# A two-layer decoder trunk in split float32: each unit of weights is placed at one of 32 byte offsets inside its tiles

## The chip, the cores and the metric

The kernel runs on one core of a Trainium2 chip. The metric is device time of one execution in microseconds (us); lower is better. A core has a matrix engine (TensorE, in the profile PE for the matmuls and PEld for the loads of the stationary operand), a vector engine (VectorE, DVE), a scalar engine (ScalarE, ACT), GpSimd (POOL) and SyncE (SP), which issues the DMAs. The engines run at the same time and wait for each other by semaphores. They share an on-chip memory of 128 partitions (SBUF); matmuls write to another one (PSUM).

## The reference

Two layers over 512 tokens of width 1024, all in float32. A layer is a token mixer (Mamba-2 SSD in the first, HGRN2 in the second), a layer norm, an MLP with squared ReLU, a second layer norm and a gated embedding:

```python
for i in range(DEPTH):
    mix = ssd_mixer(x, ...) if i % 2 == 0 else hgrn2_mixer(x, ...)
    h = layer_norm(DEEPNORM_ALPHA * x + mix, ln_g[i, 0], ln_b[i, 0])
    h = layer_norm(DEEPNORM_ALPHA * h + sq_relu_mlp(h, mlp_w1[i], mlp_w2[i]), ln_g[i, 1], ln_b[i, 1])
    x = h + jax.nn.sigmoid(h @ ple_w_gate[i]) * (p[i] @ ple_w_proj[i])
```

The bulk of it are matrix products: the input and output projections of the two mixers, the MLP (1024 to 4096 to 1024, `a = relu(h @ w1); (a * a) @ w2`) and the gates.

## The kernel before

Every product with weights is made from three matmuls. An operand is split in two parts, hi (the value rounded to the reduced format float32r) and lo (what is left), and the product is hi·hi + hi·lo + lo·hi. `mm3` (L116 to L119) issues the three; its lines L117, L118 and L119 hold most of the TensorE instructions of the profile. Each writes 128 partitions by 512 columns (some 256) of PSUM.

Weights come in units of 128 partitions by 1024 float32 values, 512 KB each. `unit` (L100 to L105) loads one into a tile `raw` of the pool `raws` (3 buffers), and `split` (L107 to L115) makes two tiles of it: ScalarE casts it into `whi` (L111), VectorE subtracts and writes `wlo` (L113). The pools `whip` and `wlop` have 5 buffers each, used in rotation, so the cast of a unit waits until TensorE has done the last matmul on the unit that had the buffer five units earlier. In the MLP some units are sums of weights, formed on VectorE in tiles `r` (`weight_sums`, L280 to L299) and split in the same way. 292 units are split in one execution.

A unit is used in one of two roles. In `project` (and `qf`) a slice of 128 columns of the unit is the stationary operand and the activations move (`pj<-b,whi` in the profile: out, moving, stationary). In `out_part`, `block_product`, the gates and `vg` the activations are stationary and a slice of 512 or 256 columns of the unit moves (`pj<-whi,b`). The activations lie in tiles of the pool `b8` (9 buffers of 8192 bytes in each partition), split in hi and lo as well. Two of the seven block operands of the MLP (`s3` and `s4`, read in `block_product`, L301) lie in tiles `blk` of the stage's own pool instead; `ones_r`, a constant, is the stationary operand of the column sums in the HGRN2 stage (L794), whose moving operand lies in `b8`.

The order of the instructions on each engine is made by a scheduler from the program's order and the priorities (`high_priority`); in the HGRN2 stage TensorE's order is written out by hand.

Where a tile lies is fixed when the program is built. The pools stand one behind the other in each partition: constants, `raws`, `whip`, `wlop`, `b8`, `acc`, `w4` (tiles a and b), small ones, a `pad` of 64 bytes, and the pool of the stage. In the program before the change:

| tiles | first byte in a partition | bytes in each | first byte modulo 256 |
|---|---|---|---|
| ones_r | 5472 | 512 | 96 |
| raw (3) | 6112 | 4096 | 224 |
| whi (5) | 18400 | 4096 | 224 (all five) |
| wlo (5) | 38880 | 4096 | 224 (all five) |
| b8 (9) | 59360 | 8192 | 224 (all nine) |
| acc | 133088 | 16384 | 224 |
| a, b | 149472, 157664 | 4096 | 224 |
| blk (2) and the other tiles of a stage | 166496 on | 8192 for blk | 96 |

The slices that a matmul takes out of these tiles begin at multiples of 512 bytes in them, so modulo 256 they begin where the tile does.

Of the kernel before, what the change touches and what calls it, by code (L numbers as in the profile page):

```python
# [9 lines left out]
F32R = mybir.dt.float32r  # L10
# [5 lines left out]
P = 128  # L16
# [26 lines left out]
def trunk(ctx: ExitStack, tc, a):  # L43
# [4 lines left out]
    whip = pool("whip", 5)  # L48
    wlop = pool("wlop", 5)
# [8 lines left out]
    psm = pool("psm", 1, space=PSUM)  # L58

    uid = [0]  # L60

    def nm(s):
        uid[0] += 1
        return f"{s}_{uid[0]}"

    def mk(p, shape, tag, dt=F32, **kw):
        return p.tile(list(shape), dt, tag=tag, name=nm(tag), **kw)

    def f32(t):
        return t.bitcast(F32)  # L70
# [29 lines left out]
    def unit(src, lead=LEAD):  # L100
        n = src.shape[1]
        with tc.high_priority(offset=lead):
            raw = mk(raws, [P, 1024], "raw")
            nc.sync.dma_start(raw[:, :n], src)
        return split(raw[:, :n], lead)  # L105

    def split(f, lead=LEAD):  # L107
        n = f.shape[1]
        with tc.high_priority(offset=lead):
            hi = mk(whip, [P, 1024], "whi", F32R)  # L110
            nc.scalar.copy(hi[:, :n], f)  # L111
            lo = mk(wlop, [P, 1024], "wlo", F32R)
            nc.vector.tensor_sub(lo[:, :n], f, f32(hi[:, :n]))  # L113
        return hi, lo

# [46 lines left out]
    cols, at = {}, 0  # L162
# [138 lines left out]
    def block_product(w, blk, first, after=None):  # L301
# [6 lines left out]
        def product(x, f, name, start, i, j):  # L308
            us = [split(v) if f in (t1, t2, t3, t4) else unit(v) for v in f]
            if start:  # L310
                banks[name] = [bank(psy, "py%d" % c) if name == "x" else bank(psj, "pj") for c in range(2)]
            t = blk[x]
            for c in range(2):
                ps = banks[name][c]
                sl = slice(c * P, (c + 1) * P)
                for k in range(4):
                    hi, lo = us[k // 2]
                    ks = slice((k % 2) * 512, (k % 2 + 1) * 512)
                    w_ = hi[:, ks], lo[:, ks]
                    mm3(ps, t[:, 0, k, sl], t[:, 1, k, sl], *w_, start and k == 0, k == 3, skip_group_check=True)  # L320
                d = acc[:, 2 * i + c, j * 512 : (j + 1) * 512]
                if (i, j) in seen:
                    nc.vector.tensor_add(d, ps, d)  # L323
                else:
                    nc.vector.scalar_tensor_tensor(d, d, ALPHA, ps, ALU.mult, ALU.add)
            seen.add((i, j))
# [719 lines left out]
```

## Time and profile before

| | |
|---|---|
| median of three timed runs | 1490.86 us (1487.89 to 1492.02) |
| the profiled execution: its own time | 1487.04 us |
| its span, first to last instruction | 1485.3 us |
| split, ScalarE (L111): 292 casts | 239.1 + 67.1 us busy |
| split, VectorE (L113): 292 subtractions | 278.5 + 78.1 us busy |
| 128x512 matmuls on weights | 5064 |
| 128x256 matmuls on weights | 1200 |
| DMA | 175.10 MB, mean 118 GB/s |

In the profile a busy time is the time in which an engine has at least one instruction under way. Matmuls overlap in TensorE's pipeline, so a matmul's own duration (389 ns in a smooth stretch) is longer than the time from its start to the start of the next one, which this document calls a step. "Idle before" is time in which the engine of that group had nothing to do just before its instructions, with what ended it. A chain of waits is the sequence of work that ended last, followed back from the last instruction.

### The profile page before, as it was taken

What the parts mean: (1) busy time and instruction counts of PE and PEld (TensorE: products, weight loads), DVE (VectorE), ACT (ScalarE), POOL (GpSimd) and SP (SyncE); (2) the same over time, 40 slices, a digit from 0 to 9 for tenths busy, and PEclk for the clock granted to TensorE, in tenths of its full rate; (3) what the DMA queues carried; (4) which work ended last, traced back from release to release, by engine and by line L of the source; (5) the groups of instructions that cost most, each with busy time, mean ns of one, the idle gap of its engine ahead of it and who ended that gap; (6) DMA issues with size and microseconds to landing.
All of it is one profiled execution on the core that took longest, in us unless ns stands there. A gap on an engine that the chain in (4) does not pass through costs nothing.

```text
span 1485.3 us, 19598 instructions
## 1 busy us (share of the span) xinstructions
PE 1463.3 (99%) x7720; PEld 1219.7 (82%) x7720; DVE 1086.6 (73%) x1672; ACT 725.3 (49%) x1020; POOL 0.9 (0%) x9
## 2 busy tenths in 40 slices
PE   8999999999999999999999999999999999999998
PEld 5888888888788888887778998989788888888777
DVE  7998677787956768687954767768786776767883
ACT  6777455563264444544534463543346454444542
POOL 0000000000000000000000000000000000000000
PEclk9999999999999999999999999999999999999999
DMA  6433223334333434444223212222423434444222
GB/s 249 159 113 101 103 97 116 100 111 141 115 114 128 156 128 145 139 154 140 80 77 102 97 58 73 71 71 86 167 90 114 142 131 152 143 142 156 99 86 72
DMA packets 48526, 175.10 MB, mean 118 GB/s; under 512 B 5393, under 2 KB 5905, under 8 KB 48305
## 3 DMA queue, kind: packets, MB, share of 16 engines
q1 hardware_dynamic: 48432, 173.84, 35.0%
q8 instruction: 61, 1.00, 0.3%
q14 instruction: 33, 0.26, 0.1%
HBM read 171.66 MB, written 2.16 MB: 117 GB/s over the span
## 4 chain that ended last, share of the span: by engine, by line
PE 92%; DVE 6%; DMA 1%; ACT 1%; issue 1%; SPq 0%; ACTq 0%
PE pj L117 24%; PE pj L118 23%; PE pj L119 23%; PE py L117 4%; PE py L118 4%; PE py L119 4%; DVE wlo L113 2%; PE py L784 1%; PE py L593 1%; PE pm L563 1%; PE py L598 1%; PE pt L208 1%; PE py L794 1%; PE py L829 1%; ACT whi L111 1%
## 5 line engine op out<-in xcount | busy, mean ns | idle before, releaser
L111 ACT CAST whi<-raw 128x1024 fp32r<-128x1024 f32 x228 | 239.1, 1049 | 329.6 <-PE pj L118 176.0
L117 PE MATMUL pj<-b,whi 128*128 128x512 f32 (+1 forms) x1024 | 391.4, 384 | 3.0 <-ACT whi L111 1.6
L113 DVE TENSOR_TENSOR wlo<-raw,whi 128x1024 fp32r<-128x1024 f32 x228 | 278.5, 1222 | 154.8 <-ACT whi L111 153.9
L118 PE MATMUL pj<-b,whi 128*128 128x512 f32 (+1 forms) x1024 | 387.7, 379 | 0.0
L119 PE MATMUL pj<-b,wlo 128*128 128x512 f32 (+1 forms) x1024 | 387.6, 379 | 0.0
L117 PE MATMUL pj<-whi,b 128*128 128x512 f32 (+1 forms) x712 | 252.0, 355 | 0.5 <-ACT sg L416 0.5
L118 PE MATMUL pj<-wlo,b 128*128 128x512 f32 (+1 forms) x712 | 249.8, 351 | 0.8 <-DVE wlo L113 0.8
L119 PE MATMUL pj<-whi,b 128*128 128x512 f32 (+1 forms) x712 | 249.8, 351 | 0.0
L117 PEld LDWEIGHTS pj<-b,whi 128*128 128x128 f32 x1024 | 192.9, 189 | 38.9 <-ACT whi L111 3.0
L119 PEld LDWEIGHTS pj<-b,wlo 128*128 128x128 f32 x1024 | 193.0, 189 | 35.7 <-DVE wlo L113 1.2
L118 PEld LDWEIGHTS pj<-b,whi 128*128 128x128 f32 x1024 | 193.2, 189 | 33.9 <-issue 1.9
L118 PEld LDWEIGHTS pj<-wlo,b 128*128 128x128 f32 x712 | 134.7, 189 | 18.2 <-DVE wlo L113 2.0
L117 PEld LDWEIGHTS pj<-whi,b 128*128 128x128 f32 x712 | 134.6, 189 | 17.8 <-ACT sg L416 0.7
L119 PEld LDWEIGHTS pj<-whi,b 128*128 128x128 f32 x712 | 134.6, 189 | 17.0 <-issue 0.2
L111 ACT CAST whi<-r 128x1024 fp32r<-128x1024 f32 x64 | 67.1, 1049 | 113.6 <-PE pj L118 90.9
L113 DVE TENSOR_TENSOR wlo<-r,whi 128x1024 fp32r<-128x1024 f32 x64 | 78.1, 1221 | 31.8 <-ACT whi L111 31.7
L119 PE MATMUL py<-whi,b 128*128 128x512 f32 x224 | 87.1, 390 | 0.0
L117 PE MATMUL py<-whi,b 128*128 128x512 f32 x192 | 75.1, 391 | 1.9 <-DVE acc L323 1.9
L118 PE MATMUL py<-wlo,b 128*128 128x512 f32 x192 | 74.7, 389 | 0.0
L498 DVE SCALAR_TENSOR_TENSOR cv<-pj,cst,cv 128x511 f32<-128x511 f32 (+2 forms) x72 | 53.3, 744 | 5.8 <-ACT cv L495 5.2
L119 PEld LDWEIGHTS py<-whi,b 128*128 128x128 f32 x224 | 42.0, 188 | 8.9 <-DVE b L394 0.3
L117 PEld LDWEIGHTS py<-whi,b 128*128 128x128 f32 x192 | 36.0, 188 | 10.7 <-DVE acc L323 3.3
(218 smaller groups left out, 1865.3 us busy)
## 6 DMA issues: line engine op xcount, KB each, us to landing
raw<-in_w SPq DMA_DIRECT2D x112, 512.0 KB, 3.5
r<-in_w SPq DMA_DIRECT2D x64, 512.0 KB, 3.8
raw<-in_wssd SPq DMA_DIRECT2D x40, 512.0 KB, 3.5
a<-csd SPq DMA_DIRECT2D x16, 512.0 KB, 4.1
raw<-in_wso SPq DMA_DIRECT2D x16, 512.0 KB, 3.5
raw<-in_wg SPq DMA_DIRECT2D x16, 512.0 KB, 3.5
raw<-in_whvg SPq DMA_DIRECT2D x16, 512.0 KB, 3.5
raw<-in_whq SPq DMA_DIRECT2D x16, 512.0 KB, 3.4
```

The source lines that it names most:

```text
L111: nc.scalar.copy(hi[:, :n], f)
L113: nc.vector.tensor_sub(lo[:, :n], f, f32(hi[:, :n]))
L117: nc.tensor.matmul(out, sh, mh, start=start, stop=False, **kw)
L118: nc.tensor.matmul(out, sh, ml, start=False, stop=False, **kw)
L119: nc.tensor.matmul(out, sl, mh, start=False, stop=stop, **kw)
L208: nc.tensor.transpose(pt[:, j * P : (j + 1) * P], src[:, k * P : (k + 1) * P], ident)
L498: nc.vector.scalar_tensor_tensor(cv[:, d:], ps[:, : T - d], convw[:, i, k : k + 1], cv[:, d:], ALU.mult, ALU.add)
L563: nc.tensor.matmul(pst_[:, c * P : (c + 1) * P], btok[:, c, :], xw[:, c].rearrange("p h q -> p (h q)"), start=True, stop=True)
L593: nc.tensor.matmul(yd[64 * r : 64 * r + 64, sl], xdt[:, 2 * c + r, :], m[:, r, sl], start=True, stop=True)
L598: nc.tensor.matmul(yo[:, c * P : (c + 1) * P], pv[:, c - 1].rearrange("p h q -> p (h q)"), cm[:, c * P : (c + 1) * P], start=True, stop=True,)
L784: nc.tensor.matmul(pc[:, sl], kk[:, sl], q[:, sl], start=True, stop=True)
L794: nc.tensor.matmul(pc[:, :n], ones_r, hl[:, r, :n], start=r == 0, stop=r == 1)
```

## The change

Each split takes the next of 32 offsets, 0 to 31 values of 4 bytes, and uses it for both of its tiles. The tiles grow by 32 values, so that a unit of 1024 still fits at the last offset. Everything that reads a unit gets the shifted view.

```diff
     uid = [0]
+    places = [0]
...
     def split(f, lead=LEAD):
         n = f.shape[1]
         with tc.high_priority(offset=lead):
-            hi = mk(whip, [P, 1024], "whi", F32R)
+            at = places[0] % 32
+            places[0] += 1
+            hi = mk(whip, [P, 1056], "whi", F32R)[:, at : at + 1024]
             nc.scalar.copy(hi[:, :n], f)
-            lo = mk(wlop, [P, 1024], "wlo", F32R)
+            lo = mk(wlop, [P, 1056], "wlo", F32R)[:, at : at + 1024]
             nc.vector.tensor_sub(lo[:, :n], f, f32(hi[:, :n]))
         return hi, lo
```

## The prediction

> **What bounds the kernel.** I read the page first: busy times, the granted clock and the chain of waits.
>
> ```profile
> span 1485.3 us, 19598 instructions
> PE 1463.3 (99%) x7720; PEld 1219.7 (82%) x7720; DVE 1086.6 (73%) x1672; ACT 725.3 (49%) x1020; POOL 0.9 (0%) x9
> ...
> PEclk9999999999999999999999999999999999999999
> ...
> PE 92%; DVE 6%; DMA 1%; ACT 1%; issue 1%; SPq 0%; ACTq 0%
> ...
> L117 PE MATMUL pj<-b,whi 128*128 128x512 f32 (+1 forms) x1024 | 391.4, 384 | 3.0 <-ACT whi L111 1.6
> ```
>
> TensorE is busy for 1463.3 of 1485.3 us at an undiminished clock and is 92% of the chain; before the largest group of matmuls on weights it idled only 3.0 us. So the time is the number of matmuls times the step from one start to the next, plus 22.0 us of idle time. Matmuls overlap, so the duration in a group's row is not that step. The windows view of a smooth stretch gives it.
>
> ```profile
> core 0: us, PE busy (x) PEld busy (x) DVE busy (x) ACT busy (x) POOL busy (x), PEclk, DMA share, GB/s
> 425.00:475.00 50.00, 50.00 (x222) 41.41 (x221) 27.81 (x34) 25.26 (x33) 0.00 (x0) 1.00 0.35 116
> ```
>
> 222 matmuls touch these 50 us. The first began before the stretch; each lasts 0.389 us, so (50.00 + 0.39)/222 = 0.227 us a step, all of them 512 columns wide.
>
> Then I looked for the same matmul with its operands at other places. Here is the timeline of TensorE where one block product starts and ends:
>
> ```profile
> 481.60 0.39 PE L118 MATMUL pj<-b,whi 128*128 128x512 f32 x1
> 481.82 0.40 PE L119 MATMUL pj<-b,wlo 128*128 128x512 f32 x1
> 482.06 0.40 PE L117 MATMUL pj<-whi,blk 128*128 128x512 f32 x1
> 482.30 0.40 PE L118 MATMUL pj<-wlo,blk 128*128 128x512 f32 x1
> 482.53 0.39 PE L119 MATMUL pj<-whi,blk 128*128 128x512 f32 x1
> ...
> 487.41 0.40 PE L119 MATMUL pj<-whi,blk 128*128 128x512 f32 x1
> 487.64 0.39 PE L117 MATMUL pj<-b,whi 128*128 128x512 f32 x1
> ```
>
> From 482.06 to 487.64 there are 24 steps on blk: 5.58/24 = 0.2325 us, 5.5 ns more than 0.227, with no wait shown. Single steps reach 0.24 us (482.06 to 482.30), and the step that leads into the first of them (481.82 to 482.06) is long as well. The work is the same as for a tile in b8; the place is not. By the program's addresses b8, whi, wlo, a and b all begin 224 bytes past a multiple of 256, and blk begins 96 past one. Its stationary operand is thus 128 bytes apart, modulo 256, from the moving one; on all other matmuls on weights the two are 0 apart. One more tile read beside b8 begins at 96: ones_r.
>
> ```profile
> L117 PE MATMUL pj<-b,whi 128*128 128x512 f32 x52 | 20.2, 389 | 0.0
> ...
> L794 PE MATMUL py<-b,ones_r 128*128 128x512 f32 x32 | 10.1, 396 | 0.0
> L117 PE MATMUL py<-whi,blk 128*128 128x512 f32 x64 | 25.3, 396 | 0.0
> ```
>
> The first row is of the smooth stretch (425 to 475 us), the others of the whole span: both tiles at 96 show 396 ns against 389, in other stages and other lines. So the trace holds two states, 0 apart and 128 apart, and the second is dearer. This is what the forecast rests on.
>
> **The change, part by part.** It adds and removes no instruction, and on every engine the order is as before. It does three things.
>
> *The writes.* 292 splits write whi (ScalarE) and wlo (VectorE, which also reads whi) at an offset of 4 bytes times a counter modulo 32.
>
> ```profile
> L111 ACT CAST whi<-raw 128x1024 fp32r<-128x1024 f32 x228 | 239.1, 1049 | 329.6 <-PE pj L118 176.0 <-PE pj L119 104.4 <-PE py L119 26.0
> L113 DVE TENSOR_TENSOR wlo<-raw,whi 128x1024 fp32r<-128x1024 f32 x228 | 278.5, 1222 | 154.8 <-ACT whi L111 153.9
> ...
> L498 DVE SCALAR_TENSOR_TENSOR cv<-pj,cst,cv 128x511 f32<-128x511 f32 x24 | 17.9, 745 | 0.2
> L498 DVE SCALAR_TENSOR_TENSOR cv<-pj,cst,cv 128x509 f32<-128x509 f32 x24 | 17.8, 742 | 5.2 <-ACT cv L495 5.2
> L605 DVE SCALAR_TENSOR_TENSOR y<-xs,cst,py 128x512 f32<-128x512 f32 x16 | 11.9, 745 | 2.3 <-PE py L593 2.2
> L266 DVE TENSOR_TENSOR blk<-a,blk 128x512 fp32r<-128x512 f32 x16 | 11.0, 685 | 0.0
> L266 DVE TENSOR_TENSOR b<-a,b 128x512 fp32r<-128x512 f32 x32 | 22.0, 686 | 4.1 <-ACT b L265 4.1
> ...
> L265 ACT CAST blk<-a 128x512 fp32r<-128x512 f32 x16 | 9.9, 617 | 2.1 <-PE pj L119 2.1
> L265 ACT CAST b<-a 128x512 fp32r<-128x512 f32 x32 | 19.8, 620 | 6.8 <-DVE a L273 4.7 <-PE py L119 1.8
> ```
>
> The convolution (L498) reads and writes 4 and 12 bytes off on VectorE, 745 and 742 ns against 745 for the even L605: no cost. Operands 128 bytes apart cost neither VectorE (685 against 686) nor ScalarE (617 against 620) anything. ScalarE at an odd word has no row; bounds: 0 by VectorE's rows, and at worst a doubling, 292 x 1.049 = 306 us more on an engine busy for 725.3, still below TensorE. I take 0. What hides it is that the splits wait for a free buffer behind TensorE (the 329.6 us before the casts); without that cover each ns on a cast is 0.3 us in all.
>
> *The tiles grow* from 4096 to 4224 bytes, which is 16 x 256 + 128. The five buffers of whi begin 224, 96, 224, 96, 224 past a multiple of 256, those of wlo 96, 224, 96, 224, 96. All that is allocated behind them moves by 1280 bytes, a whole number of 256, so b8 stays at 224, blk and ones_r at 96. The growth alone would put half of the matmuls on weights 128 apart; hi and lo of one unit are always in different states.
>
> *The reads.* 6264 matmuls read whi or wlo, 3072 as the stationary and 3192 as the moving operand (5064 are 512 wide, 1200 are 256). Buffers and offsets together spread their distance modulo 256 over all 64 words. Before, 4680 of the wide ones were 0 apart and 384 (blk) 128. Listing the built program's matmuls, 2764 of the 5064 come to lie 64 or more bytes apart (the short way round), and 3845 do so or precede one that does. The step into the first blk matmul is long as well, so I count both.
>
> The price at distances between 0 and 128 is not in the trace. Its bounds:
> - growing evenly up to 5.5 ns at 128: the mean distance is 66.4 bytes, so 5064 x 5.5 x 66.4/128 = 14.4 us, less the 384 x 5.5 = 2.1 us that blk pays already: 12.3 us;
> - 5.5 ns wherever the distance is not 0 (4964 matmuls): 27.3 - 2.1 = 25.2 us;
> - 5.5 ns from half way on, both steps counted: 3845 x 5.5 = 21.1, less 2.1: 19.0 us;
> - the slowest step on blk, 0.24 against 0.227, everywhere: 4964 x 13 ns = 64.5, less 2.1: 62 us;
> - nothing at all: 0.
>
> I take 19 us: it uses the mean that was measured, and it lies between the first two. The narrow matmuls:
>
> ```profile
> L118 PE MATMUL pj<-wlo,b 128*128 128x256 f32 x272 | 76.8, 282 | 0.0
> ...
> L794 PE MATMUL py<-b,ones_r 128*128 128x256 f32 x16 | 3.1, 276 | 0.0
> ...
> L882 PE MATMUL py<-a,cm 128*128 128x128 f32 x64 | 11.0, 274 | 0.0
> L884 PE MATMUL py<-pv,xs 128*128 128x128 f32 x48 | 9.3, 275 | 0.0
> ```
>
> At 256 columns the pair 128 apart (ones_r) lasts 276 ns against 282, and at 128 columns a and cm, 128 apart, last 274 against 275 for pv and xs, 0 apart. So I put the 1200 narrow ones at 0; the ends are -6 ns (-7 us) and 5.5 ns (+7 us).
>
> The Trainium skill bears on this: "TensorE: Matmul & The Clock Gate", section "Step-by-step: what each phase is for", says that TensorE reads SBUF through two independent ports, one for the moving operand and one for the weight load. By that rule the distance could not matter and the sum would be 0; the blk steps of 0.2325 us against 0.227 speak against it, and the measurement decides.
>
> **Sum.** The profiled execution took 1487.0 us (span 1485.3), 3.8 below the median of 1490.86. 1487.0 + 19 = 1506.0; on the median's footing 1510.
>
> **Rivals.**
> *No effect.* The long steps belong to something else that blk and ones_r share (their absolute place, which does not change), and the offset as such is free as on VectorE. For it: the narrow rows. Against it: half the weight buffers come to lie at 96 too. 1491 us.
>
> *Faster.* A step has a fixed part, which distance 0 may make large:
>
> ```profile
> 406.43 0.28 PE L118 MATMUL pj<-b,whi 128*128 128x256 f32 x1
> ...
> 408.34 0.28 PE L118 MATMUL pj<-b,whi 128*128 128x256 f32 x1
> ```
>
> 16 steps in 1.91 us are 119 ns for 256 columns; 227 for 512 leaves 227 - 2 x (227 - 119) = 11 ns that do not grow with the width. If those are the weight read, begun at the same place as the moving read, being held up by it, then the distances with no such clash save up to 11 ns. It decides if more than half of the distances are free: 6264 x 11 x 0.5 = 34 us, 1456 us. Against it: at 128 apart the wide step is longer, not shorter.
>
> *Much slower.* Distances in between, or starts off a multiple of 16 bytes (2394 moving and 2304 stationary operands), cost more than 128 apart: at the slowest blk step everywhere 1491 + 62 = 1553 us. For it: 0.24 us does occur. Against it: the mean on blk is 0.2325.
>
> **How the numbers follow.** Forecast 0.62, its own range 1500 to 1525 (12 to 34 us); much slower 0.17; no effect 0.13; faster 0.08. A change under 0.3%, 4.5 us, can't be told from none here. Slower 0.79, same 0.13, faster 0.08. The range 1488 to 1552 takes in no effect and most of the dear case; outside stay the gain (0.08) and the dearer half of that rival (0.09).
>
> **What would show it.** Right: idle time on TensorE stays near 22 us while smooth stretches hold fewer matmuls (some 218 instead of 222 in 50 us); the step changes from unit to unit and stays near 0.227 where the operands are almost 0 apart; L111 and L113 keep 1049 and 1222 ns. Wrong: steps of 0.227 throughout (no effect), steps below 0.22 (faster), most at 0.24 or above (much slower), or longer casts that TensorE waits for, which I have put at nothing.

## The result and the profile after

| | before | after |
|---|---|---|
| median | 1491.44 us (4 runs, 1487.89 to 1493.23) | 1509.58 us (4 runs, 1508.86 to 1512.19) |
| ratio after / before | | 1.0134, 95% interval 1.0120 to 1.0147 |
| the profiled execution: own time, span | 1487.04, 1485.3 us | 1510.05, 1508.0 us |

The kernel became slower by 1.34%, 20 us of 1491.4. The forecast was 1510 us on the median's footing, where 1509.58 was measured, and 1506.0 for the profiled execution, which took 1510.05. The page of the changed kernel has these lines (busy time, share and count of each engine; the clock; the chain of waits; groups of instructions). The lines of code stand three further down than before: L120 to L122 are the three matmuls, L114 and L116 the split.

```profile
span 1508.0 us, 19598 instructions
PE 1485.9 (99%) x7720; PEld 1223.2 (81%) x7720; DVE 1086.8 (72%) x1672; ACT 724.5 (48%) x1020; POOL 0.9 (0%) x9
...
PEclk9999999999999999999999999999999999999999
...
PE 94%; DVE 4%; DMA 1%; ACT 1%; issue 1%; SPq 0%; ACTq 0%
...
L114 ACT CAST whi<-raw 128x1024 fp32r<-128x1024 f32 x228 | 238.9, 1048 | 344.2 <-PE pj L121 185.3
...
L116 DVE TENSOR_TENSOR wlo<-raw,whi 128x1024 fp32r<-128x1024 f32 x228 | 278.6, 1222 | 165.6 <-ACT whi L114 164.8
```

The 22.7 us that the span gained are busy time of TensorE: 1485.9 - 1463.3 = 22.6. Some 3 us of them are clock (an estimate): the mean granted clock was 0.999 in the profiled execution before and 0.997 in the one after, 0.002 x 1508. Executions of before with a lower granted clock are longer (medians in the runs below: 1489.8 us at 0.999, 1491.5 at 0.997, 1494.2 at 0.995), so a span alone is a poorer measure of the change than the ratio. VectorE and ScalarE do the same work in the same time (1222 and 1048 ns for a piece of a split, 1222 and 1049 before); they only wait longer for buffers, 344.2 us instead of 329.6 before the casts. The number of matmuls is the same, 7720. In the smooth stretch that the prediction used, the granted clock is 1.00 as before (third column from the end), and 216 matmuls touch it instead of 222:

```profile
425.00:475.00 50.00, 50.00 (x216) 40.44 (x215) 28.79 (x37) 26.74 (x36) 0.00 (x0) 1.00 0.35 115
```

So the step between matmuls grew. Two smooth stretches of the timeline, first and last matmul of each:

```profile
423.16 0.39 PE L120 MATMUL pj<-b,whi 128*128 128x512 f32 x1
...
456.45 0.39 PE L122 MATMUL pj<-b,wlo 128*128 128x512 f32 x1
...
235.64 0.39 PE L120 MATMUL pj<-whi,b 128*128 128x512 f32 x1
...
254.26 0.39 PE L122 MATMUL pj<-whi,b 128*128 128x512 f32 x1
```

In the first, weights are stationary: 143 steps in 33.29 us, 232.8 ns. In the second they move: 80 steps in 18.62 us, 232.75 ns. Before, both kinds took 227. This is the step that the prediction read off blk (232.5 ns).

For the rest of this document I take from each trace the start of every wide (512 columns) matmul on weights to the start of the next matmul, leave out those of 270 ns and more (waits), and give means. Before: 228.0 ns over 4821 steps; after: 232.7 over 4823. The narrow ones (256 columns, steps under 200 ns) went from 119.8 to 119.1.

### The profile page after: what moved, and what is told of

It reads as the page before. It is cut to its first block, busy times and chain, and to the rows that moved or that the text cites. A ratio compares the mean times of both kernels' runs of the same rounds, so it can differ in the third digit from the quotient of the medians.

```text
span 1508.0 us, 19598 instructions
## 1 busy us (share of the span) xinstructions
PE 1485.9 (99%) x7720; PEld 1223.2 (81%) x7720; DVE 1086.8 (72%) x1672; ACT 724.5 (48%) x1020; POOL 0.9 (0%) x9
## 4 chain that ended last, share of the span: by engine, by line
PE 94%; DVE 4%; DMA 1%; ACT 1%; issue 1%; SPq 0%; ACTq 0%
PE pj L120 24%; PE pj L121 24%; PE pj L122 24%; PE py L120 4%; PE py L122 4%; PE py L121 4%; PE py L787 1%; PE py L596 1%; DVE wlo L116 1%; PE pm L566 1%; PE py L601 1%; ACT whi L114 1%; PE py L797 1%; PE pt L211 1%; PE py L832 1%; DVE b L215 1%
## 5 line engine op out<-in xcount | busy, mean ns | idle before, releaser
L114 ACT CAST whi<-raw 128x1024 fp32r<-128x1024 f32 x228 | 238.9, 1048 | 344.2 <-PE pj L121 185.3
L120 PE MATMUL pj<-b,whi 128*128 128x512 f32 (+1 forms) x1024 | 395.8, 388 | 2.9 <-ACT whi L114 1.6
L116 DVE TENSOR_TENSOR wlo<-raw,whi 128x1024 fp32r<-128x1024 f32 x228 | 278.6, 1222 | 165.6 <-ACT whi L114 164.8
L121 PE MATMUL pj<-b,whi 128*128 128x512 f32 (+1 forms) x1024 | 392.0, 383 | 0.0
L122 PE MATMUL pj<-b,wlo 128*128 128x512 f32 (+1 forms) x1024 | 392.0, 383 | 0.0
L120 PE MATMUL pj<-whi,b 128*128 128x512 f32 (+1 forms) x712 | 254.2, 358 | 0.5 <-ACT sg L419 0.5
L122 PE MATMUL pj<-whi,b 128*128 128x512 f32 (+1 forms) x712 | 251.5, 353 | 0.0
L120 PEld LDWEIGHTS pj<-b,whi 128*128 128x128 f32 x1024 | 193.2, 189 | 42.8 <-ACT whi L114 3.2
L122 PEld LDWEIGHTS pj<-b,wlo 128*128 128x128 f32 x1024 | 193.3, 189 | 39.8 <-DVE wlo L116 1.2
L120 PEld LDWEIGHTS pj<-whi,b 128*128 128x128 f32 x712 | 134.4, 189 | 19.3 <-ACT sg L419 0.7
L122 PEld LDWEIGHTS pj<-whi,b 128*128 128x128 f32 x712 | 134.5, 189 | 18.7 <-issue 0.2
L114 ACT CAST whi<-r 128x1024 fp32r<-128x1024 f32 x64 | 67.2, 1049 | 117.7 <-PE pj L121 93.9
L116 DVE TENSOR_TENSOR wlo<-r,whi 128x1024 fp32r<-128x1024 f32 x64 | 78.1, 1221 | 34.8 <-ACT whi L114 34.7
L122 PE MATMUL py<-whi,b 128*128 128x512 f32 x224 | 88.2, 395 | 0.0
L120 PE MATMUL py<-whi,b 128*128 128x512 f32 x192 | 76.0, 396 | 1.8 <-DVE acc L326 1.8
L122 PEld LDWEIGHTS py<-whi,b 128*128 128x128 f32 x224 | 42.2, 188 | 10.0 <-DVE b L397 0.3
L120 PEld LDWEIGHTS py<-whi,b 128*128 128x128 f32 x192 | 36.1, 188 | 11.2 <-DVE acc L326 2.6
```

The lines of the kernel that those rows point to most:

```text
L120: nc.tensor.matmul(out, sh, mh, start=start, stop=False, **kw)
L121: nc.tensor.matmul(out, sh, ml, start=False, stop=False, **kw)
L122: nc.tensor.matmul(out, sl, mh, start=False, stop=stop, **kw)
```

## The experiments

Theories: **A**, the step is 227 ns where a matmul's two operands start at the same place modulo 256 and dearer at another distance; **B**, the absolute place counts; **C**, the change of place from unit to unit counts; **W**, starts that are not multiples of 16 bytes cost. All times are compared with the kernel before on the same chip.

| run | ratio, 95% interval | weights stationary | weights move, b8 stationary | weights move, blk stationary | narrow |
|---|---|---|---|---|---|
| before | | 227.6 | 227.7 | 232.8 | 119.8 |
| the change | 1.0134 (1.0120 to 1.0147) | 232.3 | 233.0 | 233.0 | 119.1 |
| E1 growth alone | 1.0087 (1.0072 to 1.0102) | 231.4 | 230.8 | 230.8 | 118.6 |
| E2 offsets alone | 1.0128 (1.0113 to 1.0143) | 232.1 | 232.9 | 233.7 | 119.3 |
| E3 weights 128 off | 1.0107 (1.0092 to 1.0122) | 232.7 | 232.8 | 227.5 | 118.7 |
| E4 all 128 off | 1.0001 (0.9991 to 1.0010) | 227.6 | 227.6 | 232.8 | 120.0 |
| E5 0 or 256 off | 0.9998 (0.9988 to 1.0008) | 227.6 | 227.7 | 232.8 | 119.8 |
| E6 weights 4 off | 1.0211 (1.0197 to 1.0225) | 232.4 | 237.3 | 236.3 | 121.6 |
| E7 weights 12 off | 1.0066 (1.0051 to 1.0082) | 231.1 | 229.2 | 230.7 | 117.3 |
| E8 blk and ones_r at 0 | 0.9993 (0.9984 to 1.0002) | 227.6 | 227.6 | 226.8 | 119.5 |
| E9 b8 4 off | 1.0196 (1.0180 to 1.0212) | 237.3 | 232.4 | 232.6 | 119.7 |
| E10 weights and b8 4 off | 1.0299 (1.0281 to 1.0317) | 237.6 | 237.6 | 236.3 | 122.5 |
| E11 as E8, narrow weights 12 off | 0.9958 (0.9943 to 0.9972) | 227.6 | 227.6 | 226.8 | 117.3 |

The four middle columns are mean steps in ns; in bytes, "off" is against the place before.

### E1 and E2: which part of the edit, the growth or the offsets

Both are edits to the changed kernel.

```diff
-            at = places[0] % 32
+            at = 0
```

> The tiles of whi and wlo grow to 4224 bytes as in the change, but every unit stays at offset 0. Of the 5064 wide matmuls on weights 2344 are then 128 bytes apart modulo 256 from their other operand and 2720 are 0 apart. Theory A (distance: any wide matmul whose two operands are not 0 apart, or that stands beside one, takes about 5.5 ns more): hi and lo of a unit are always in different states, so nearly every step is beside one; +15 to +25 us, a ratio of 1.010 to 1.017. Theory W (word place: the cost comes from starts that are not multiples of 16 or 32 bytes): no such start exists here; ratio 1.000. Theory C (change of place from unit to unit): places change in whole 128s; between the two.

```diff
-            hi = mk(whip, [P, 1056], "whi", F32R)[:, at : at + 1024]
+            hi = mk(whip, [P, 1088], "whi", F32R)[:, at : at + 1024]
...
-            lo = mk(wlop, [P, 1056], "wlo", F32R)[:, at : at + 1024]
+            lo = mk(wlop, [P, 1088], "wlo", F32R)[:, at : at + 1024]
```

> The 32 offsets as in the change, but in tiles of 4352 bytes (17 x 256), so that the growth adds no distance of 128: the distances are the offsets alone, 0 to 124 bytes, the same for hi and lo of a unit. Theory A with any distance other than 0 priced alike: +22 to +27 us, 1.015 to 1.018. Theory A with a price that grows evenly to 5.5 ns at 128: +13 us, 1.009. Theory W: the whole of the change, 1.013.

E1 gave 1.0087 and E2 1.0128, so either part alone makes most of the loss, and together they cost no more than the offsets alone. W by itself is out: in E1 every start is a multiple of 16 bytes. E1 came in just under what A promised (1.010 to 1.017). E2 lies under A's 1.015 to 1.018 as well and on W's 1.013, so its time alone doesn't tell the two apart. Its steps with weights stationary do: there every moving operand starts at a multiple of 16 bytes, and they grew all the same.

The trace of E1 tells which neighbours count. Where weights are stationary, by the state (0 or 128 apart) of the matmul before, the matmul itself and the one after, the mean steps are: 0,0,0 227.8 ns (471 steps); 1,0,0 228.9 (338); 0,0,1 232.4 (364); 0,1,0 233.3 (309). So a step is dear when its own matmul or the next one is off, and not on account of the one before. Where weights move the picture is less clear (229.6 for 0,0,0 on b8).

E2 gives the price by distance that the trace of before lacked. With weights stationary: 228.4 ns at offset 0 (111 steps), 232.0 at 4 to 28 bytes (610), 232.3 at 32 to 60 (737), 233.1 at 64 to 92 (502), 231.6 at 96 to 124 (581). In the mean the price is there from the first 4 bytes on and does not grow.

It is a mean, though, and not due at every distance. Take the stretches of at least 12 such steps on one unit, without their last three, which lead into the next unit. Of the 87 at an offset other than 0, five took under 228 ns a step: both at 120 bytes, two of the five at 36 bytes (the other three took 233 to 235 ns), and one of the four at 16 bytes. The first of the two at 120 bytes, its first and last matmul in E2:

```profile
437.79 0.39 PE L120 MATMUL pj<-b,whi 128*128 128x512 f32 x1
...
443.00 0.40 PE L122 MATMUL pj<-b,wlo 128*128 128x512 f32 x1
```

23 steps in 5.21 us are some 227 ns, as at distance 0. So a distance other than 0 costs 4 to 5 ns in the mean, but what decides it for a single unit is open.

### E3 and E4: distance or absolute place

E3 puts 128 unused bytes ahead of whi and 128 behind wlo; E4 leaves out the second.

```diff
+    pad1 = pool("pad1", 1)
     whip = pool("whip", 5)
     wlop = pool("wlop", 5)
+    pad2 = pool("pad2", 1)
     b8 = pool("b8", 9)
...
+    nc.gpsimd.memset(mk(pad1, [P, 32], "pad1"), 0.0)
+    nc.gpsimd.memset(mk(pad2, [P, 32], "pad2"), 0.0)
```

> No offsets and tiles of 4096 bytes as before, but 128 unused bytes ahead of whi and 128 behind wlo: every wide matmul on weights beside b8 is 128 apart, always the same. Theory A: 4680 steps at 0.2325 instead of 0.227 us and 384 (blk, now 0 apart) the other way: +23.6 us, 1.016. Theory W: 1.000. Theory C: 1.000, since nothing changes from unit to unit.

> 128 unused bytes ahead of whi, nothing behind wlo: whi, wlo, b8, acc, a, b and the tiles of a stage all move by 128 bytes, so all distances are as before (ones_r alone comes to be 0 apart from b8, blk stays 128 apart). Theory A (distance): 1.000. Theory B (the absolute place of an operand, 96 past a multiple of 256 being the dear one): the 4680 wide matmuls on b8 go to 0.2325 us, +25 us, 1.016, and the 384 on blk to 0.227 us.

The same stretch of the timeline in E3, first and last of 144 matmuls:

```profile
424.74 0.39 PE L119 MATMUL pj<-b,whi 128*128 128x512 f32 x1
...
457.97 0.40 PE L121 MATMUL pj<-b,wlo 128*128 128x512 f32 x1
```

and in E4:

```profile
420.60 0.40 PE L118 MATMUL pj<-b,whi 128*128 128x512 f32 x1
...
453.05 0.39 PE L120 MATMUL pj<-b,wlo 128*128 128x512 f32 x1
```

E3: 33.23 us for 143 steps, 232.4 ns. E4: 32.45 us, 226.9 ns. In E3 blk changed sides: 227.5 ns, while everything beside b8 went to 232.7. In E4 weights and activations moved together, every wide operand changed its absolute place, and neither a step nor the time moved. B is out. C is out as the only cause: nothing varies in E3. The ratio of E3, some 16 us, lies below the 1.016 expected, 23.6 us. The price per step explains little of that: beside b8 the wide steps grew by 5.1 ns and on blk they fell by 5.3, 4680 x 5.1 - 384 x 5.3 = 21.8 us, and the narrow ones, 1.1 ns shorter, take 1.3 us off. That sums of steps exceed the measured times comes back at the end.

### E5: a change of place by whole 256s

```diff
-            at = places[0] % 32
+            at = 64 * (places[0] % 2)
```

(in the wider tiles of E2)

> Places change from unit to unit, by 0 or 256 bytes, in tiles of 4352 bytes (17 x 256): the buffers and the offsets differ by whole 256s, so every distance is 0 modulo 256 as before (blk 128), while no two neighbouring buffers start at the same place modulo 512. Theory A (distance modulo 256): 1.000. Theory C (a change of place from unit to unit costs by itself) or a period of 512 instead of 256: 1.008 to 1.013.

0.9998, and every mean as before. Moving units about is free as long as the distance stays a multiple of 256. With E3 this also bounds the period: 128 is dear and 256 is not.

### E6, E7, E9, E10: the word at which the moving operand starts

In the changed kernel the wide steps with moving weights depended on the start modulo 16 bytes: 232.1 ns at 0, 236.4 at 4, 233.7 at 8, 230.0 at 12 (some 570 steps each), while with stationary weights they lay between 232.0 and 233.0 whatever the word. Four kernels test that. E6 and E7 have `at = 1` and `at = 3` for all units in the tiles of E2. E9 shifts the activations instead, E10 both:

```diff
+    def act():
+        return mk(b8, [P, 2112], "b8", F32R)[:, 1:2049]
...
-            self.hi = [mk(b8, [P, 4, T], "b8", F32R) for _ in range((n + 3) // 4)]
+            self.hi = [act().rearrange("p (k t) -> p k t", k=4) for _ in range((n + 3) // 4)]
...
```

> A constant offset of 4 bytes for every unit, in tiles of 4352 bytes: the distance is 4 or 252 throughout, and every moving weight operand starts 4 bytes past a multiple of 16. Theory A with one price for every distance but 0: +20 to +25 us, 1.013 to 1.017, equal to the run with 12 bytes. Theory A+W (distance, and on top of it the word at which the moving operand starts; in the changed kernel wide steps with moving weights took 236.6 ns at 4 bytes past 16 and 229.8 at 12 past): about 236 ns where weights move, 232 where they are stationary, +33 us, 1.022.

> A constant offset of 12 bytes for every unit, otherwise as the run with 4 bytes. Theory A with one price: 1.013 to 1.017, equal to the run with 4 bytes. Theory A+W: about 230 ns where weights move, 232 where they are stationary, +16 us, 1.011, so the two runs differ by some 15 us.

> The weights stay where they were; every activation tile of b8 starts 4 bytes further (in buffers of 8448 bytes, 33 x 256). The distances are 4 or 252 as in the run with a constant 4 bytes, but now the moving operand is 4 past a multiple of 16 where weights are stationary, and a multiple of 16 where weights move. Theory A+W, W being about the moving operand: the other way round from that run, about 237 ns where weights are stationary and 232 where they move, 1.022 to 1.026. If the word place of the weight tile itself counts (in whatever role): 237 where weights move, or nowhere.

> Weights and b8 both start 4 bytes further: the distance is 0 again, but every moving operand is 4 past a multiple of 16. Theory A alone, with no cost of the word place: 1.000 to 1.001, steps of 0.227 us. Theory A+W with W added to A: 227 + 4.7 = 231.7 ns on all wide steps, +22 us, 1.015. If any start off 16 costs as much as a distance does: 237 ns, 1.03.

E6, first 81 matmuls with moving weights, then 144 with stationary ones:

```profile
238.37 0.40 PE L120 MATMUL pj<-whi,b 128*128 128x512 f32 x1
...
257.34 0.40 PE L122 MATMUL pj<-whi,b 128*128 128x512 f32 x1
...
426.85 0.40 PE L120 MATMUL pj<-b,whi 128*128 128x512 f32 x1
...
460.08 0.39 PE L122 MATMUL pj<-b,wlo 128*128 128x512 f32 x1
```

E9, the same two stretches:

```profile
238.07 0.39 PE L117 MATMUL pj<-whi,b 128*128 128x512 f32 x1
...
256.66 0.39 PE L119 MATMUL pj<-whi,b 128*128 128x512 f32 x1
...
426.91 0.41 PE L117 MATMUL pj<-b,whi 128*128 128x512 f32 x1
...
460.86 0.40 PE L119 MATMUL pj<-b,wlo 128*128 128x512 f32 x1
```

E6: 237.1 ns (80 steps) where the weights move, 232.4 (143 steps) where they are stationary. E9, with the activations shifted: 232.4 and 237.4, just the other way round. So it is the start of the moving operand that costs, whichever tensor moves. E10 has distance 0 again, but for the 480 wide matmuls on blk, a and b, and every moving operand at 4 past 16:

```profile
429.86 0.40 PE L117 MATMUL pj<-b,whi 128*128 128x512 f32 x1
...
463.86 0.40 PE L119 MATMUL pj<-b,wlo 128*128 128x512 f32 x1
```

237.8 ns over 143 steps, and the slowest kernel of all, 1.0299. Of the three cases that I had written down, no cost of the word (227 ns) and A and W adding (231.7) were wrong. The third, 237 ns and 1.03, came out, but not for its reason, that any start off 16 costs as much as a distance: at 12 bytes it doesn't (E7). At 4 past 16 the step is 237 at distance 0 (E10) as at a distance of 252 (E6, E9). Where the moving operand starts at a multiple of 16, distance decides between 227 and 232; at 8 and 12 bytes no run has distance 0. E6 came out as expected (1.022). E9 stayed under its 1.022 to 1.026, though its steps were as expected; of the nine executions of before on its chip, five were granted 0.994 or 0.995 of the clock, and E9's 0.997 or 0.998. E7 missed on the good side: at 12 bytes moving weights take 229.2 ns, less than distance alone takes at a multiple of 16, and 1.0066 is well under the 1.011 expected.

### E8 and E11: from the rule to a faster kernel

E8 brings the last two tiles to distance 0.

```diff
-    nc.gpsimd.memset(mk(pad, [P, 16], "pad"), 0.0)
+    nc.gpsimd.memset(mk(pad, [P, 48], "pad"), 0.0)
...
+    nc.gpsimd.memset(mk(cpool, [P, 32], "gap0"), 0.0)
     ones_r = mk(cpool, [P, P], "ones_r", F32R)
+    nc.gpsimd.memset(mk(cpool, [P, 32], "gap1"), 0.0)
```

> No offsets; blk and ones_r are brought to distance 0 from b8 as well, by unused bytes (128 more in the pad ahead of a stage's tiles, 128 ahead of ones_r and 128 behind it). Theory A: the 384 wide matmuls on blk and the 32 on ones_r go from 0.2325 to 0.227 us, -2.3 us, a ratio of 0.9985, faster than both kernels. If blk is slow for another reason: 1.000, steps on blk at 0.2325 us.

The first block product on blk in E8, with the matmul that follows it:

```profile
486.04 0.39 PE L117 MATMUL pj<-whi,blk 128*128 128x512 f32 x1
...
491.25 0.39 PE L119 MATMUL pj<-whi,blk 128*128 128x512 f32 x1
491.48 0.39 PE L117 MATMUL pj<-b,whi 128*128 128x512 f32 x1
```

24 steps in 5.44 us are 226.7 ns, where the prediction read 232.5 before: the steps did what A says. The time, 0.9993, can't be told from 1 by its interval, nor from the 0.9985 expected.

E11 adds a constant 12 bytes for 24 units that are read 256 columns at a time, by 1152 of the 1200 narrow matmuls (`at=3` for the calls of `unit` in `vg` and in the first half-width projections of `hidden`, 0 for all others, in the tiles of E2).

> The kernel with all wide matmuls at distance 0 (unused bytes ahead of the stage's tiles and around ones_r), and 24 units that are read 256 columns at a time (v and g of the HGRN2 stage, the first half-width projections of the two MLPs) at a constant 12 bytes. In the run with 12 bytes throughout the narrow steps took 117.2 ns against 119.8 before. Theory: 1200 narrow steps less 2.6 ns, -3 us, and -2.3 us of blk and ones_r: 1486, 0.9965. If the narrow gain was only that of the phase they happened to have: 0.999.

The narrow matmuls with moving weights (by shape; busy us, mean ns), first E8:

```profile
L117 PE MATMUL pj<-whi,b 128*128 128x256 f32 x272 | 78.1, 287 | 0.5 <-ACT sg L416 0.5
L119 PE MATMUL pj<-whi,b 128*128 128x256 f32 x272 | 77.0, 283 | 0.0
```

then E11:

```profile
L117 PE MATMUL pj<-whi,b 128*128 128x256 f32 x272 | 77.0, 283 | 0.5 <-ACT sg L416 0.5
L119 PE MATMUL pj<-whi,b 128*128 128x256 f32 x272 | 76.0, 279 | 0.0
```

Each lasts 4 ns less, and the mean step of all narrow ones went from 119.5 to 117.3 ns, 1200 x 2.2 = 2.6 us. E11 took 1486.04 us against 1493.78 on the same chip, 0.9958, with the expected 0.9965 within its interval. A part of that is clock, since five of the nine executions of before there were granted 0.994 or 0.995, and E11's 0.996 to 0.999. Of those granted 0.997 or more, four of before took 1489.9 to 1491.5 us and four of E11 1485.4 to 1488.6, 4.2 us between the medians. So it is faster than both kernels, by some 0.3%; the steps make 1200 x 2.5 + 384 x 6.0 = 5.3 us of it against before.

## Why the prediction was right, point by point

- *TensorE sets the end, so the time is steps times matmuls.* Right: the span grew by 22.7 us, TensorE's busy time by 22.6, and its idle time stayed at 22.1 (22.0 before). Summed by kind: 2688 wide steps with stationary weights x 4.7 ns (227.6 to 232.3) = 12.6; 1992 on b8 or a, b with moving ones x 5.3 (227.7 to 233.0) = 10.6; blk 384 x 0.2 = 0.1; 1200 narrow x -0.7 = -0.8. Together 22.5 us. The ratio makes 20 us of it; why the steps sum to more is open (see the end).
- *The writes cost nothing.* Right: 1048 and 1222 ns a piece, as before, and the cover was not needed.
- *Two places in the trace of before (blk, ones_r) show a dear distance.* Right, and shown to be distance and not place: E3 and E4, and E8, where blk got cheap. One of the readings didn't support it. The 396 ns of blk and ones_r are means of the whole span, the 389 beside them the mean of a smooth stretch. Over the whole span matmuls on b8 last as long, 397 ns in the largest group (first line). What shows the difference are the steps, and blk's row in E8 (second line), 396 before. ones_r, among narrow matmuls, fell only to 393 there.

```profile
L117 PE MATMUL pj<-b,whi 128*128 128x512 f32 x896 | 355.7, 397 | 1.6 <-ACT whi L111 1.6
...
L117 PE MATMUL py<-whi,blk 128*128 128x512 f32 x64 | 24.9, 389 | 0.0
```

- *Both the matmul that is off and the step that leads into it count.* Right for stationary weights (E1: 233.3 and 232.4 ns against 227.8); unclear for moving ones.
- *The price, 5.5 ns, counted on 3845 of 5064 steps.* That the sum came so near is in part luck, by errors against each other. The price does not start half way to 128: E2 has it from 4 bytes on, so most of the 4964 steps at a distance pay it, and the sign that steps stay near 227 where the operands are almost 0 apart did not come (232.0 at 4 to 28 bytes). In the mean it is a little less than 5.5 ns: 5.1 in E3, with everything beside b8 128 apart, and 4.7 with stationary and 5.3 with moving weights in the change. By the steps, 22.5 us, 19 was too low, and the measured time then grew by less than the steps.
- *The growth.* I gave it weight, since it alone puts half of the matmuls 128 apart. Alone it does cost 0.87% (E1), but behind the offsets it adds nothing that shows (E2).
- *The rival with starts off a multiple of 16 bytes.* Put at 0.17 as a way to 1553 us. Its mechanism is real (E6, E9, E10), but it is a matter of which word: 236.4 ns at 4, 230.0 at 12, in the changed kernel about 1 ns in the mean over the four, and only on the matmuls whose moving operand is a weight.
- *No effect, and faster.* Neither: the fastest run of 24 wide steps in the changed kernel has a mean of 226.8 ns, no less than at distance 0. The reasoning for *faster* (distance 0 might be the bad one) is refuted for wide matmuls by E3. Narrow ones, which the prediction put at 0 with an end of -6 ns, did get 0.7 ns shorter, and 1.1 in E3.
- *Two independent read ports.* The Trainium skill, "TensorE: Matmul & The Clock Gate", section "Step-by-step: what each phase is for", has the moving operand and the weight load read through two independent ports. If that meant that the places of the two operands do not matter to each other, this case would not agree: E3 against E4 (232.4 against 226.9 ns) shows that they do.

## What to carry to other kernels

In a kernel that TensorE bounds, where tiles lie is part of the tuning: here a smooth run of wide float32r matmuls took 227 ns a step with both operands at the same place modulo 256, 232 in the mean at another distance, and 237 with the moving operand 4 bytes past a multiple of 16. Size and order tiles so that the operands of wide matmuls share one residue modulo 256, and look at the addresses again after any edit that changes a tile's size, even by a few bytes. To find such a loss, compare steps (start to start) of equal matmuls on different tiles: it shows as no wait anywhere, only as busy time.

## What the runs showed that I had not expected

- The price of a distance is, in the mean, a step and not a slope: 228.4 ns at offset 0, 232.0 at 4 to 28 bytes (E2). Single units at a distance run as fast as at 0, and why is open.
- 4 bytes past 16 cost the moving operand 10 ns a step even at distance 0 (E10: 237.6 against 227.6), 12 bytes 1.5 with the distance included (E7: 229.2), and the narrow matmuls even gain at 12: 117.3 ns against 119.5 (E11 against E8). Why the words differ was not settled.
- What happens inside TensorE was not shown either. Where they are dear the steps run through a pattern (228 to 241 ns in the product on blk that the prediction shows), which would fit two reads that get in each other's way, but no run here takes one of the two reads away.
- Sums of steps exceed the measured times: 22.5 us against 20 for the change, and in E10 5064 wide steps x 9.5 ns and 1200 narrow x 2.7, 51 us, against 45 (46 beside executions of before with a like granted clock). In E10 the steps of 270 ns and more, which hold the waits, sum to 96.2 us, and to 102.2 before, so slower matmuls may hide some of TensorE's own waits. In the change the same sum is 102.1, so for it the gap of 2.5 us is open.
